# Inverse squared key norms of the RWKV-7 heads: one reciprocal per token and head, spread by TensorE, in place of one per row

## The chip, the cores and the metric

The kernel runs on one core of one Trainium2 chip. The metric is the device time of one execution in microseconds (us); the number quoted is the median of several runs.

## The reference, cut to what matters

One decoder layer: an xLSTM mLSTM group beside an RWKV-7 group, then cross-attention into a fixed memory and a SwiGLU FFN, over 2048 tokens of width 1024. The change lies in the RWKV-7 group (8 heads of 64), where the key direction is normalised per token and head:

```python
kk = hs(k * k_k)                                  # (token, head, 64)
kk = kk / jnp.maximum(jnp.sqrt(jnp.sum(kk * kk, -1, keepdims=True)), 1e-12)
a = hs(a)
k = hs(k) * (1.0 + (a - 1.0) * hp(k_a))
y = rwkv7_scan(r, hs(decay), k, v, -kk, kk * a)
```

The kernel keeps `kk` without its norm on one side of a product (`KB`) and puts the whole inverse square, 1 / max(sum, 1e-24), on the other (`RR`), so no root is taken.

## The kernel before, in words

The program runs through five stages: a pre-pass (norm, transposes, small projections, to about 118 us), the mixer (to about 1190 us), output projection, attention, and the FFN. The change touches the mixer and a constant.

`mixer` (L647) works through 16 steps: two halves of the heads (`hq`) by 8 groups of 256 tokens. For each step `prepare` (L311) runs twice, for `e` = 0 and 1, on a tile of 128 channels (two heads of 64 on the partition axis) by 256 tokens: 32 prepares in all. Beside it stand the triangular `solve` on GpSimd (L408), its `join` on TensorE (L441), the chunked `scan` (L467) and the `mlstm` group (L537), one step behind. From the second step on the big projections (`qps`, `vops` of mlstm, `kps`, `rps`, `vps` of prepare; lines 53 to 55, three fp16 passes each) are there to fill TensorE.

Channels lie on partitions, so the sum over a head's 64 channels is a matmul: `sq` (L355, ScalarE) is the squared key, and L357 multiplies it by `c.bones`, a 128x128 matrix of two 64x64 blocks of ones. That gives `sps`, in which every one of a head's 64 rows holds the same sum. VectorE then takes the maximum with 1e-24 (L359), the reciprocal (L360) and the product with `k` (L361), all on 128x256, and L364 scales the result twice into `RR`. `RR` and `KB` are the operands of `aps` (L393), whose masked copies `MX`, `RR`, `AY` (L397 to L399) feed the solve and the scan. `bps` (L379, the bonus term, `ta` from L377) and `vps` (L383, the transposed and centred `v`) share the two-buffer PSUM pool `pax` (tag `ax`) with `wps`, `sps`, `aps` and `kbps`.

A later part of each step is `tps` (L516): TensorE transposes the scan's output `y` after GpSimd has scaled it (L511, L512). `pps` (L457) is the first matmul of `join` and waits for the solve's result, fetched from DRAM as `T`.

The order of instructions on every engine is set by the scheduler of the tile framework, which simulates a timeline; each engine then runs its list in order. An edit of the source can thus move instructions well away from it.

Of the kernel before, what the change touches and what calls it, by code (L numbers as in the profile page):

```python
# [7 lines left out]
F32 = mybir.dt.float32  # L8
F16 = mybir.dt.float16
AF = mybir.ActivationFunctionType  # L10
ALU = mybir.AluOpType
# [4 lines left out]
P = 128  # L16
# [68 lines left out]
def col(c, r):  # L85
    return c.par[:, r:r + 1]
# [19 lines left out]
def rwkv_consts(c, pool, I):  # L106
    nc = c.nc
    par = c.par
    c.mu_s = pool.tile([P, 14], F32, name="mu_s")
    nc.vector.tensor_scalar(c.mu_s, par[:, R_MU:R_MU + 14], DSC, None, op0=ALU.mult)  # L110
    c.mu_c = pool.tile([P, 14], F32, name="mu_c")
    nc.vector.tensor_scalar(c.mu_c, par[:, R_MU:R_MU + 14], -DSC, DSC, op0=ALU.mult, op1=ALU.add)
    c.bones = pool.tile([P, P], F32, name="bones")
    nc.vector.memset(c.bones, 0.0)
    nc.vector.memset(c.bones[0:64, 0:64], 1.0)
    nc.vector.memset(c.bones[64:128, 64:128], 1.0)

    c.cent = pool.tile([P, P], F32, name="cent")
    nc.vector.scalar_tensor_tensor(c.cent, c.bones, -1.0 / 64, c.ident, op0=ALU.mult, op1=ALU.add)
    c.mask = pool.tile([P, P], F32, name="mask")  # L120
    nc.gpsimd.memset(c.mask, 1.0)
    for b in (0, 64):
        nc.gpsimd.affine_select(c.mask[b:b + 64, 0:64], c.mask[b:b + 64, 0:64], [[1, 64]], ALU.is_gt, 0.0,
                                base=0, channel_multiplier=-1)
        nc.gpsimd.affine_select(c.mask[b:b + 64, 64:128], c.mask[b:b + 64, 64:128], [[1, 64]], ALU.is_ge, 0.0,
                                base=0, channel_multiplier=-1)
    c.restart = pool.tile([P, 4, 64], F32, name="restart")
    nc.gpsimd.memset(c.restart, 1.0)
    nc.gpsimd.memset(c.restart[:, :, 0:1], 0.0)
    c.gmix = pool.tile([P, 8], F32, name="gmix")  # L130
    nc.vector.tensor_scalar(c.gmix, par[:, R_GMIX:R_GMIX + 8], SW, None, op0=ALU.mult)
# [115 lines left out]
def mixer_pass(c, I, hq, tp, T):  # L247

    nc, tc = c.nc, c.tc
    SGN = 256  # L250
# [35 lines left out]
    def shifted(ps, j, e, o):  # L286
        m = 4 * j + 2 * hq + e
        t = tp.t2.tile([P, SGN], F32, tag="tmu", name="tmu", bufs=2)
        nc.scalar.activation(t, ps[:, 0:SGN], AF.Copy, scale=c.mu_s[:, m:m + 1])
        nc.scalar.activation(o, ps[:, 1:SGN + 1], AF.Copy, scale=c.mu_c[:, m:m + 1])  # L290
        nc.vector.tensor_tensor(o, o, t, ALU.add)
        return o
# [18 lines left out]
    def prepare(sg, e, u, G):  # L311
# [34 lines left out]
        k = shifted(ps, 1, e, tp.t2.tile([P, SGN], F32, tag="k", name="k"))  # L346
# [6 lines left out]

        sq = tp.t1.tile([P, SGN], F32, tag="tA", name="sq")
        nc.scalar.activation(sq, k, AF.Square, scale=col(c, R_KK + ct))  # L355
        sps = tp.pax.tile([P, SGN], F32, tag="ax", name="sps")
        nc.tensor.matmul(sps, lhsT=c.bones, rhs=sq, start=True, stop=True)  # L357
        sq = tp.t1.tile([P, SGN], F32, tag="tA", name="sq")
        nc.vector.tensor_scalar(sq, sps, 1e-24, None, op0=ALU.max)  # L359
        nc.vector.reciprocal(sq, sq)  # L360
        nc.vector.tensor_tensor(sq, sq, k, ALU.mult)  # L361
        sq = sq.rearrange(v4, n=4)
        for h, b in enumerate(halves):
            nc.vector.scalar_tensor_tensor(RR[b, :, h, 0:64], sq[b], c.kk[b, 0, ct:ct + 1], E[b, :, 0:64],  # L364
                                           op0=ALU.mult, op1=ALU.mult)
# [3 lines left out]
                                       op0=ALU.mult, op1=ALU.mult)  # L369
# [257 lines left out]
    def load_u(sg):  # L627
# [13 lines left out]
    p = Ctx()  # L641
    p.weights, p.load_u, p.group, p.prepare, p.solve, p.join, p.scan, p.mlstm, p.st = \
        weights, load_u, group, prepare, solve, join, scan, mlstm, st
    return p

# [739 lines left out]
def build(tc, I, out, dbg=None):  # L1385
# [5 lines left out]
    with ExitStack() as ctx:  # L1391
# [15 lines left out]
        with ExitStack() as mix:  # L1407
            rc = mix.enter_context(tc.tile_pool(name="rc", bufs=1, side="right"))
            c.zg = rc.tile([P, 8, NC], F32, name="zg")
            rwkv_consts(c, rc, I)  # L1410
            pre_pass(c, I, T, rc)
            mlstm_gates(c, mix, I, T)
            mixer(c, I, T)
# [51 lines left out]
```

## Time and profile before

| what | us |
|---|---|
| median of 3 runs | 3042.4 (3040.26 to 3044.18) |
| the profiled execution, its own time | 3042.23 |
| its span in the profile | 3040.4 |
| TensorE busy / VectorE / ScalarE / GpSimd | 2892.4 / 2092.2 / 1251.0 / 1145.8 |

The span is what the trace covers; 1.8 us of the execution lie around it. "PE" is TensorE's matmuls, "PEld" its weight loads, DVE VectorE, ACT ScalarE, POOL GpSimd. A float32 matmul of the program shows as two records with a weight load each, so 32 `sps` matmuls are 64 records; a float32 transpose shows as one. Matmul records overlap, because the end of one is modelled with its drain; what a matmul costs TensorE is the distance from its start to the start of the next one, and not its duration.

### The profile page before, as it was taken

The page shows a single profiled execution, that of the slowest core. Times are in us where ns is not written, and L with a number is a line of the kernel's source. Part 1 is how long each engine was busy: PE and PEld are TensorE (multiplying, and loading weights), DVE is VectorE, ACT ScalarE, POOL GpSimd, SP SyncE. Part 2 cuts the span into 40 slices and gives each one's busy share as a digit, 9 for nine tenths or more (in the row PEclk, how much of TensorE's full clock was granted, in tenths as well). Part 3 has the DMA queues.
Part 4 walks back from the last instruction along what each step waited for, and adds up shares of the span by engine and source line. Part 5 has one row for each costly group of instructions (what it writes and reads, how often), then busy time and mean ns, then how long its engine had stood idle before and what let it go on. Part 6 is the DMA issues. An engine that isn't in the chain of part 4 may idle for free. (4 is left out here: it accounts for less than half of the span.)

```text
span 3040.4 us, 53763 instructions
## 1 busy us (share of the span) xinstructions
PE 2892.4 (95%) x20259; PEld 1797.2 (59%) x20259; DVE 2092.2 (69%) x3853; ACT 1251.0 (41%) x2859; POOL 1145.8 (38%) x1830
## 2 busy tenths in 40 slices
PE   7779999998999998999999998999999999899998
PEld 4568888887888887655455543444444444344443
DVE  6557777777777776564588886544545546888975
ACT  6434444555444445453466652222222223423432
POOL 3064654465555444132111153222222222644542
PEclk9889999999999999999999999999999999999999
DMA  8512222333112214554223365111111212554441
GB/s 266 141 50 62 48 50 53 83 77 88 48 46 52 50 38 129 187 177 139 87 91 132 119 245 173 56 56 56 56 59 57 61 60 70 181 180 151 156 141 72
DMA packets 328833, 307.25 MB, mean 101 GB/s; under 512 B 88846, under 2 KB 278524, under 8 KB 327676
## 3 DMA queue, kind: packets, MB, share of 16 engines
q1 hardware_dynamic: 328572, 303.81, 32.6%
q8 instruction: 160, 2.62, 0.4%
q14 instruction: 101, 0.83, 0.1%
HBM read 208.23 MB, written 95.49 MB: 100 GB/s over the span
## 5 line engine op out<-in xcount | busy, mean ns | idle before, releaser
L53 PE MATMUL pp<-u,wb 128*128 128x512 f16 x1232 | 468.2, 380 | 13.7 <-DVE e L1170 8.2
L54 PE MATMUL pp<-u,wb 128*128 128x512 f16 x1232 | 468.1, 380 | 0.0
L55 PE MATMUL pp<-u,wb 128*128 128x512 f16 x1232 | 467.9, 380 | 0.0
L1170 DVE TENSOR_TENSOR e<-pp,e 128x512 f32<-128x512 f32 x308 | 208.5, 689 | 302.3 <-PE pp L55 288.4
L432 POOL TENSOR_TENSOR tmp<-M,X 64x126 f32<-64x126 f32 (+22 forms) x496 | 193.9, 391 | 165.4 <-DMA M<-md 131.0
L55 PE MATMUL dps<-w,gS 128*128 128x512 f16 x616 | 234.1, 380 | 8.6 <-DVE gS L49 8.5
L54 PE MATMUL dps<-w,gS 128*128 128x512 f16 x616 | 234.0, 380 | 1.7 <-DVE w L49 1.7
L53 PE MATMUL dps<-w,gS 128*128 128x512 f16 x616 | 234.1, 380 | 0.0
L434 POOL TENSOR_TENSOR X<-X,tmp 64x126 f32<-64x126 f32 (+22 forms) x496 | 204.9, 413 | 35.8
L54 PEld LDWEIGHTS <-wb 128*128 128x128 f16 x1232 | 120.8, 98 | 155.3 <-issue 11.5
L53 PEld LDWEIGHTS <-wb 128*128 128x128 f16 x1232 | 120.8, 98 | 151.9 <-DMA u<-u_d 6.0
L55 PEld LDWEIGHTS <-wb 128*128 128x128 f16 x1232 | 120.8, 98 | 146.4 <-issue 1.5
L1186 POOL TENSOR_TENSOR S<-raw 128x512 f32<-128x512 f32 x22 | 33.8, 1537 | 414.2 <-DVE wb L49 414.2
L53 PE MATMUL qps<-uh,wh 128*128 128x259 f16 x512 | 141.9, 277 | 14.4 <-ACT wh L48 5.6
L54 PEld LDWEIGHTS <-wh 128*128 128x128 f16 x1280 | 128.9, 101 | 30.3 <-issue 11.6
L53 PEld LDWEIGHTS <-wh 128*128 128x128 f16 x1280 | 127.5, 100 | 25.4 <-ACT wh L48 7.0
L55 PE MATMUL qps<-uh,wl 128*128 128x259 f16 x512 | 141.1, 277 | 1.0 <-DVE wl L49 1.0
L54 PE MATMUL qps<-ul,wh 128*128 128x259 f16 x512 | 140.9, 276 | 0.0
L53 PE MATMUL vops<-wh,uh 128*128 128x256 f16 x512 | 139.7, 273 | 0.2
L55 PE MATMUL vops<-wh,ul 128*128 128x256 f16 x512 | 139.7, 273 | 0.0
L54 PE MATMUL vops<-wl,uh 128*128 128x256 f16 x512 | 139.6, 273 | 0.0
L55 PEld LDWEIGHTS <-wl 128*128 128x128 f16 x1280 | 126.4, 99 | 20.9 <-DVE wl L49 1.9
(423 smaller groups left out, 7677.2 us busy)
## 6 DMA issues: line engine op xcount, KB each, us to landing
g_d<-e SPq DMA_DIRECT2D x88, 256.0 KB
h<-h_d SPq DMA_DIRECT2D x32, 512.0 KB
acc<-h_d SPq DMA_DIRECT2D x32, 512.0 KB
u_d<-ub SPq DMA_DIRECT2D x56, 256.0 KB
wraw<-in_w_in_dram SPq DMA_DIRECT2D x48, 256.0 KB
ga<-g_d SPq DMA_DIRECT2D x32, 384.0 KB
raw<-in_ffn_w_gate_dram SPq DMA_DIRECT2D x22, 512.0 KB
raw<-in_ffn_w_up_dram SPq DMA_DIRECT2D x22, 512.0 KB
```

Source lines behind the costliest of these rows:

```text
L53: nc.tensor.matmul(out, lhsT=lhs[0], rhs=rhs[0], start=start, stop=False)
L54: nc.tensor.matmul(out, lhsT=lhs[0], rhs=rhs[1], start=False, stop=False)
L55: return nc.tensor.matmul(out, lhsT=lhs[1], rhs=rhs[0], start=False, stop=stop)
L432: nc.gpsimd.tensor_tensor(tv, M[:, s, s + 1:32].unsqueeze(2).to_broadcast(shp), X[:, s, 0:ncl].unsqueeze(1).to_broadcast(shp), ALU.mult)
L434: nc.gpsimd.tensor_tensor(X[:, s + 1:32, 0:ncl], X[:, s + 1:32, 0:ncl], tv, ALU.add)
L1170: add = lambda o, x, y: nc.vector.tensor_tensor(o, x, y, ALU.add)
L1186: nc.gpsimd.tensor_tensor(s[0], a[1][0], a[1][1], ALU.add)
```

## The change

The sums are formed the other way round: `sq` becomes the stationary operand, in two slices of 128 tokens, and a new constant `c.ind` (128x2, ones where a row belongs to the head) the moving one. `sps` is then 128 tokens by 4 (two token slices by two heads). Maximum and reciprocal run on 128x4. ScalarE repeats each value 64 times into `rcb` (128x256), and two matmuls with `rcb` as stationary operand and the identity as moving one bring it back to channels by tokens, `rb`, in PSUM. VectorE multiplies `rb` by `k`. Line numbers of the changed kernel are 4 higher from L117 on and 12 higher from L361 on.

```diff
@@ rwkv_consts
     nc.vector.memset(c.bones[64:128, 64:128], 1.0)
+    c.ind = pool.tile([P, 2], F32, name="ind")
+    nc.vector.memset(c.ind, 0.0)
+    nc.vector.memset(c.ind[0:64, 0:1], 1.0)
+    nc.vector.memset(c.ind[64:128, 1:2], 1.0)
@@ prepare
         sq = tp.t1.tile([P, SGN], F32, tag="tA", name="sq")
         nc.scalar.activation(sq, k, AF.Square, scale=col(c, R_KK + ct))
-        sps = tp.pax.tile([P, SGN], F32, tag="ax", name="sps")
-        nc.tensor.matmul(sps, lhsT=c.bones, rhs=sq, start=True, stop=True)
+        sps = tp.pax.tile([P, 4], F32, tag="ax", name="sps")
+        for m in range(2):
+            nc.tensor.matmul(sps[:, 2 * m:2 * m + 2], lhsT=sq[:, m * P:(m + 1) * P], rhs=c.ind, start=True, stop=True)
+        rc = tp.t1.tile([P, 4], F32, tag="rc", name="rc")
+        nc.vector.tensor_scalar(rc, sps, 1e-24, None, op0=ALU.max)
+        nc.vector.reciprocal(rc, rc)
+        rcb = tp.t1.tile([P, 4, 64], F32, tag="tA", name="rcb")
+        nc.scalar.copy(rcb, rc.unsqueeze(2).to_broadcast([P, 4, 64]))
+        rb = tp.pax.tile([P, SGN], F32, tag="ax", name="rb")
+        for m in range(2):
+            nc.tensor.matmul(rb[:, m * P:(m + 1) * P], lhsT=rcb[:, 2 * m:2 * m + 2].rearrange("p h d -> p (h d)"), rhs=c.ident,
+                             start=True, stop=True)
         sq = tp.t1.tile([P, SGN], F32, tag="tA", name="sq")
-        nc.vector.tensor_scalar(sq, sps, 1e-24, None, op0=ALU.max)
-        nc.vector.reciprocal(sq, sq)
-        nc.vector.tensor_tensor(sq, sq, k, ALU.mult)
+        nc.vector.tensor_tensor(sq, rb, k, ALU.mult)
```

**How the order moves, first place: TensorE and ScalarE in the second of the four prepares of steps 0 and 1.** Little is there yet to fill TensorE. `rps` and `vps` (L53 to L55) are projections of the prepare after it; `ch` belongs to the scan. TensorE before:

```order
L55 LDWEIGHTS wl
L55 MATMUL rps<-uh,wl 128x257
L473 MATMUL ch<-VS,RR_1579 64x64
L357 MATMUL sps<-sq,bones 128x256
L379 MATMUL bps<-ta,bones 128x256
L383 MATMUL vps<-cent,v 128x128 x2
L53 LDWEIGHTS wh
L53 MATMUL vps<-uh,wh 128x257
```

TensorE now:

```order
L55 MATMUL rps<-uh,wl 128x257
L485 MATMUL ch<-VS,RR_1583 64x64 x2
L362 MATMUL sps<-ind,sq 128x2 x2
L370 MATMUL rb<-ident,rcb 128x128 x2
L391 MATMUL bps<-ta,bones 128x256
L53 LDWEIGHTS wh
L53 MATMUL vps<-uh,wh 128x257
```

ScalarE now (L385 is the copy inside `KB`, L373 before):

```order
L341 ACTIVATE En<-L_1946 128x256
L345 ACTIVATE E<-L_1946 128x4x64
L359 ACTIVATE sq<-k,par 128x256
L385 COPY KB<-KB 128x4x64
L367 COPY rcb<-rc 128x256
L294 ACTIVATE r<-rps,mu_c 128x256
```

Here `rb` stands directly behind `sps` and ahead of `bps`: nothing lies between them, and `rcb` comes behind the copy inside `KB`.

**Second place: TensorE and VectorE in an `e` = 1 prepare of the second half of the heads** (the sequence repeats there from step to step). TensorE now, around `rb`; between the last `sps` and these rows stand 20 of the fp16 matmuls of `qps`, and some small ones of `join` (`xps`) and mlstm (`skp`):

```order
L55 LDWEIGHTS wl
L55 MATMUL qps<-uh,wl 128x259
L489 MATMUL ch<-R,MX_1596 128x64
L370 MATMUL rb<-ident,rcb 128x128 x2
L391 MATMUL bps<-ta,bones 128x256
L489 MATMUL ch<-R,MX_1596 128x64
L606 MATMUL ncp<-vx,Em 128x129
```

VectorE before:

```order
L587 TENSOR_TENSOR kt<-skp,tk 128x256
L372 TENSOR_TENSOR KB<-ta,En 128x4x64
L377 SCALAR_TENSOR_TENSOR ta<-r,par,ta 128x256
L359 TENSOR_SCALAR sq<-sps 128x256
L360 RECIPROCAL sq<-sq 128x256
L380 TENSOR_TENSOR bon<-bps,v 128x256
L598 SCALAR_TENSOR_TENSOR Cn<-Cn,dec,ncp 128x129
L361 TENSOR_TENSOR sq<-sq,k 128x256
L364 SCALAR_TENSOR_TENSOR RR_1582<-sq,kk,E 64x4x64 x2
```

VectorE now:

```order
L389 SCALAR_TENSOR_TENSOR ta<-r,par,ta 128x256
L625 SCALAR_TENSOR_TENSOR r<-r,ss 128x2
L364 TENSOR_SCALAR rc<-sps 128x4
L365 RECIPROCAL rc<-rc 128x4
L597 TENSOR_TENSOR Em<-Em,skp 128x256
L599 TENSOR_TENSOR kt<-skp,tk 128x256
L373 TENSOR_TENSOR sq<-rb,k 128x256
L392 TENSOR_TENSOR bon<-bps,v 128x256
L376 SCALAR_TENSOR_TENSOR RR_1586<-sq,kk,E 64x4x64 x2
```

The scheduler has put other work between `rc` and `sq` on VectorE, and between `sps` and `rb` on TensorE. From the third step on 20 to 32 fp16 matmuls stand between `sps` and `rb`, except in the two `e` = 0 prepares of steps 2 and 3, which have scan and mlstm work there. The list of DMAs (SyncE) has as many entries as before.

## Rows read from the trace of the kernel before

**Rows 1.** The page, part 1: busy time, share and records of each engine.

```profile
PE 2892.4 (95%) x20259; PEld 1797.2 (59%) x20259; DVE 2092.2 (69%) x3853; ACT 1251.0 (41%) x2859; POOL 1145.8 (38%) x1830
```

**Rows 2.** Windows: stretch, length, busy of PE, PEld, DVE, ACT, POOL; PEclk, DMA, GB/s.

```profile
120.00:200.00 80.00, 55.73 (x362) 43.89 (x361) 54.85 (x128) 32.33 (x82) 32.91 (x75) 0.83 0.32 60
245.00:575.00 330.00, 326.36 (x3535) 283.71 (x3534) 256.12 (x633) 159.72 (x469) 178.17 (x415) 1.00 0.22 52
827.00:1086.00 259.00, 245.38 (x2667) 214.04 (x2666) 191.99 (x478) 122.12 (x359) 138.16 (x319) 1.00 0.20 47
```

**Rows 3.** Waits of PE in 245 to 575 us: total us, times, longest.

```profile
PE tps L516 <- POOL y L512: 3.3, 5, 1.1
```

**Rows 4.** Waits of PE in 827 to 1110 us.

```profile
PE tps L516 <- POOL y L512: 6.2, 4, 2.0
PE qps L53 <- ACT cv L556: 4.6, 5, 1.2
PE qps L53 <- ACT r L290: 4.2, 5, 0.9
```

**Rows 5.** Waits of PE in 120 to 200 us.

```profile
PE bps L379 <- DVE ta L377: 11.3, 4, 3.3
```

**Rows 6.** Single lines, the norm: ns min/median/max of one, first and last start.

```profile
L359 DVE TENSOR_SCALAR sq<-sps x32: 393/416/425, 124.3 to 1122.5; 128x256 f32<-128x256 f32 x32
L360 DVE RECIPROCAL sq<-sq x32: 1733/1742/1753, 125.2 to 1123.0; 128x256 f32<-128x256 f32 x32
L361 DVE TENSOR_TENSOR sq<-sq,k x32: 402/420/583, 127.4 to 1125.2; 128x256 f32<-128x256 f32 x32
```

**Rows 7.** Single lines, nearest kin of the new operations.

```profile
L606 DVE RECIPROCAL r<-r x32: 144/158/167, 232.1 to 1184.8; 128x2 f32<-128x2 f32 x32
L611 DVE TENSOR_SCALAR ss<-ss x32: 157/169/279, 233.2 to 1189.8; 128x2 f32<-128x2 f32 x32
L373 ACT COPY KB<-KB x32: 404/405/425, 125.3 to 1122.1; 128x256 f32<-128x256 f32 x32
```

**Rows 8.** Timeline of PE, full mixer: start, us, engine, line, operation.

```profile
400.14 0.56 PE L477 MATMUL ch<-R,MX 128*128 128x64 f32 x4
400.54 0.28 PE L54 MATMUL qps<-ul,wh 128*128 128x259 f16 x1
400.65 0.59 PE L379 MATMUL bps<-ta,bones 128*128 128x256 f32 x2
401.08 0.61 PE L383 MATMUL vps<-cent,v 128*128 128x128 f32 x4
401.52 0.28 PE L55 MATMUL qps<-uh,wl 128*128 128x259 f16 x1
```

**Rows 9.** Timeline of PE in the pre-pass: the thinnest matmuls there.

```profile
62.42 0.17 PE L54 MATMUL gps<-wg,uh 128*128 128x8 f16 x1
62.44 0.17 PE L55 MATMUL gps<-wg,ul 128*128 128x8 f16 x1
```

**Rows 10.** Timeline of PE and DVE, second prepare, and the first join.

```profile
145.80 0.70 PE L357 MATMUL sps<-sq,bones 128*128 128x256 f32 x2 [3.17 <-ACT sq L355]
147.06 0.42 DVE L359 TENSOR_SCALAR sq<-sps 128x256 f32<-128x256 f32 x1
149.39 0.39 DVE L377 SCALAR_TENSOR_TENSOR ta<-r,par,ta 128x256 f32<-128x256 f32 x1
149.83 1.22 PE L379 MATMUL bps<-ta,bones 128*128 128x256 f32 x2 [3.33 <-DVE ta L377]
...
204.06 1.38 PE L457 MATMUL pps<-T,MX 32*32 32x32 f32 x32 [4.92 <-DMA T<-t1d]
```

**Rows 11.** Timeline of PE and DVE, a late prepare, and DVE before a late wait.

```profile
862.61 0.70 PE L357 MATMUL sps<-sq,bones 128*128 128x256 f32 x2
863.35 0.42 DVE L359 TENSOR_SCALAR sq<-sps 128x256 f32<-128x256 f32 x1
863.81 1.75 DVE L360 RECIPROCAL sq<-sq 128x256 f32<-128x256 f32 x1
869.52 1.95 PE L393 MATMUL aps<-RR,KB 128*128 128x128 f32 x16
...
908.00 0.06 DVE L340 MEMSET E<- 128x4 f32 x1 [2.47 <-POOL W L342]
```

## The prediction

> **What bounds the kernel now.** I began with the totals of the engines: TensorE is busy for 95% of the span, VectorE for 69%, ScalarE and GpSimd for about 40% [rows 1]. The change touches the mixer only, so the second view is the windows by stage. From 245 to 575 us TensorE has a matmul in flight for 326.4 of 330 us at the full granted clock of 1.00, and VectorE works for 256 us, or 78%; from 827 to 1086 us TensorE has 245.4 of 259 us and VectorE 192.0, or 74% [rows 2]. So VectorE, which the change relieves, has a fifth to a quarter of its time free in both, and TensorE, which gets more work, has almost none. In the start of the mixer, 120 to 200 us, TensorE is busy for 55.7 of 80 us at a mean clock of 0.83 [rows 2]: there chains of single operations decide.
>
> The third view says what ends TensorE's idle time. Up to 575 us it is one wait, `tps` for GpSimd's scaled `y`, 3.3 us in five steps [rows 3]. From 827 us it is 6.2 us for the same, 4.6 us for a ScalarE copy `cv` and 4.2 us for ScalarE's `r` [rows 4]. No wait for the norm, its product or `RR` is among them. The fourth view, the timeline, gives the price of a matmul as the distance between starts.
>
> **The change part by part.**
>
> VectorE. Taken away in each of 32 prepares: the maximum of 0.42 us and the reciprocal of 1.74 us [rows 6]. Added: both on 128x4, of which the nearest rows are a reciprocal on 128x2 of 0.16 us and a scalar operation on 128x2 of 0.17 us [rows 7]. The product with `k` stays at 0.42 us [rows 6], now reading `rb`. That is 2.16 - 0.33 = 1.83 us less per prepare and 59 us less in all, 3.7 us per step. I put it at nothing in the sum where TensorE is full, since VectorE has slack there [rows 2] and the waits that TensorE still has start elsewhere: before the late `r` and `tps` VectorE itself stands still, 2.47 us, for GpSimd's copy `W` [rows 11], which comes out of GpSimd's triangular solve. What it may be worth if I am wrong is a rival.
>
> ScalarE. One copy of 128x256 more, 0.41 us by its kin inside `KB` [rows 7], 13 us in all. ScalarE has half its time free [rows 2], so it costs only as part of the chain, below.
>
> TensorE. The old `sps` is one float32 matmul of 256 columns in two passes. Its twin `bps`, with the same operands' shapes, starts at 400.65 and the next matmul at 401.08: 0.43 us [rows 8]. The way back, `rb`, is two float32 matmuls of 128 columns; `vps` is the same, four passes from 401.08 to 401.52: 0.44 us [rows 8]. The new sums are four passes of 2 columns with a fresh 128x128 float32 stationary operand each. The trace has no such row, so it is bounded. The nearest is `ch` (L477), float32, the same stationary size, 64 columns: four passes from 400.14 to 400.54, 0.10 us each [rows 8]. The other end is `gps`, fp16 with 8 columns, 0.02 to 0.03 us from start to start [rows 9]. With 128 columns a pass takes 0.11 us and with 64 still 0.10 us, so a float32 pass hardly gets cheaper with fewer columns, and the load seems to set its price: I take 0.10, 0.40 us for four. At the other end it is 0.10 us for four. Hence 0.40 + 0.44 - 0.43 = +0.41 us per prepare, between +0.11 and +0.45.
>
> The Trainium skill, TensorE: Matmul & The Clock Gate, section LDWEIGHTS (loading the stationary operand), says that a load costs its number of columns over 1.2 GHz, whatever streams past it afterwards: an estimate from it of 0.107 us a pass makes +0.44 us per prepare, against the +0.11 us that `gps` would give. By that rule, the `ch` row agrees and thin matmuls are no saving here, which speaks against this change.
>
> Of the 32 prepares, 28 lie where TensorE is full, from step 2 on: 28 x 0.41 = **+11.5 us**.
>
> The chain. `rb` waits for VectorE's reciprocal and ScalarE's copy, and `bps` stands behind it in TensorE's list. In a late prepare the maximum starts 0.74 us and the reciprocal 1.20 us after `sps` [rows 11]; with the short operations `rc` is ready near 1.2 us and `rcb` 0.41 us later, say 2 us with the hand-overs. Between `sps` and `rb` the scheduler has put 20 fp16 matmuls at 0.11 us (the distance from 400.54 to 400.65 [rows 8]), 2.2 us, with small float32 ones besides. So it is covered, by one microsecond or less. And `RR`, after `rb`, has until `aps`, which came 6.9 us after `sps` before [rows 11]; I cost the chain at nothing.
>
> The start. In the four prepares of steps 0 and 1 nothing covers it. Before, `sps` starts at 145.80 and TensorE idles 3.33 us until `bps` at 149.83, because `ta` (L377) stands behind the long reciprocal on VectorE [rows 10]; the four such waits make 11.3 us [rows 5]. Now, from the maximum's start at 147.06 [rows 10]: 0.17 + one 128x256 operation of 0.42 + 0.16 on VectorE, then two copies of 0.41 on ScalarE, then `rb` with 0.44, is 149.07 without hand-overs. `bps` comes up to 0.76 us earlier, or no earlier with hand-overs and a lower clock. I take 0.5 us. Only two prepares count: behind the other two lies TensorE's wait of 4.92 us for the first solve [rows 10], which takes up what they gain. **-1.0 us**, between +2 and -2.5.
>
> What fills a wait. In steps 2 to 7 the new passes fall partly between the scan's output and `tps`, where TensorE waits for GpSimd anyway [rows 3]. At most 3.3 us come back; I take **-2.5 us**. In the second half the list between the two is no longer than before, and I take nothing of [rows 4].
>
> After the mixer no operation changes, and the four new memsets run at the start beside DMAs.
>
> The sum is +11.5 - 1.0 - 2.5 = +8.0 us on the profiled execution of 3042.2 us. That stands 0.2 us under the median of 3042.4, so 3050 us either way. A measurement here tells about 0.2% from no change, 6 us; the forecast lies just beyond it. Its own range runs from 28 x 0.11 with both gains at their fullest, 3.1 - 2.5 - 3.3 = -2.7, to 28 x 0.45 with +2 and none of the fill, +14.6: 3039 to 3057 us.
>
> **The rivals.**
>
> VectorE's relief shortens the steps: faster. If TensorE's late waits for `cv` and `r`, 8.8 us in five steps [rows 4], are owed to a late VectorE, then relief of 3.7 us per step removes them, 1.8 us in each of seven second-half steps, 12 us. With the 6.2 and 3.3 us for `tps` [rows 3, 4] that is -22 in the place of -2.5, and 11.5 - 1.0 - 22 makes about 3031 us. It decides when more than 17 us of TensorE's waits go. For it: VectorE is the second busiest engine in the mixer. Against it: before two of these waits it stood idle itself [rows 11]. Chance 0.17, at 3031 to 3036 us.
>
> TensorE has room that its busy row hides: no change. The Trainium skill, Perfetto Trace Analysis, section Identifying the Most-Contended Engine, holds matmul busy time a bad measure and the busy share of weight loads the good one. That share is 283.7 of 330 us here, 86% [rows 2]. If the added passes slip into the rest, and with the -3.5 us of the other terms, the time is about 3039; if half of them do, 3044. Against it: starts follow each other without a gap in [rows 8]. Chance 0.20, at 3038 to 3045 us.
>
> `rb` waits: slower still. Were the chain 0.5 us longer than its cover in each of 28 prepares, TensorE would stand 14 us more, with `bps` and all that follows behind it: 3064 us. It decides from a `sps` to `rcb` time of some 2.2 us on. For it: the cover is thin and VectorE runs its list in order, so one late wait ahead of `rc` is passed on. Chance 0.08.
>
> **How the numbers follow.** The forecast has 0.55. Of its range some two thirds lie more than 6 us above the time before, so slower is 0.37 + 0.08 = 0.45; same is the remaining 0.18 with the second rival's 0.20, 0.38; faster is 0.17. The range that holds 8 in 10 leaves out half of the fast rival and the upper part of the last: 3035 to 3058 us.
>
> **What would show it right or wrong.** Right: VectorE's busy time falls to about 2033 us and ScalarE's rises to 1264; four thin passes of `sps` take 0.4 us from start to start and `rb` 0.44; steps in 245 to 575 us get longer by some 0.8 us; waits of `tps` there shrink. Wrong: thin passes at 0.03 us, waits of PE for `rcb` in the full stretches, or late waits for `cv`, `r` and `tps` that are gone.

## The result, and the profile after

The changed kernel takes 3061.5 us (median of 3 runs, 3058.3 to 3062.9) where the kernel before takes 3042.4: a ratio of 1.0055, with a 95% interval of 1.0041 to 1.0068. It is slower by 19 us, above the range that was forecast. The profiled execution took 3058.3 us with a span of 3056.6, 16.2 us longer than the span before.

The page, part 1, of the changed kernel, and its windows (columns as in [rows 2]):

```profile
PE 2911.3 (95%) x20451; PEld 1822.3 (60%) x20451; DVE 2046.0 (67%) x3856; ACT 1257.4 (41%) x2891; POOL 1144.7 (37%) x1830
...
120.00:200.00 80.00, 54.14 (x368) 44.46 (x369) 46.81 (x122) 32.55 (x85) 30.95 (x71) 0.80 0.33 60
245.00:575.00 330.00, 326.07 (x3557) 286.09 (x3554) 234.76 (x629) 159.92 (x476) 172.55 (x400) 1.00 0.21 51
830.00:1090.00 260.00, 254.49 (x2723) 222.78 (x2721) 182.66 (x480) 121.96 (x368) 138.12 (x322) 1.00 0.22 53
```

VectorE is 46 us less busy, and nothing came of it; TensorE is 19 us busier and the span 16 us longer. In the full stretches TensorE has about as little idle time as before, or less. The single lines of the new operations (columns as in [rows 6]) have the durations that were taken from their kin:

```profile
L364 DVE TENSOR_SCALAR rc<-sps x32: 142/154/163, 123.6 to 1135.1; 128x4 f32<-128x4 f32 x32
L365 DVE RECIPROCAL rc<-rc x32: 161/178/178, 124.2 to 1135.3; 128x4 f32<-128x4 f32 x32
L367 ACT COPY rcb<-rc x32: 390/403/404, 124.6 to 1135.5; 128x256 f32<-128x256 f32 x32
L373 DVE TENSOR_TENSOR sq<-rb,k x32: 352/424/426, 126.3 to 1138.5; 128x256 f32<-128x256 f32 x32
```

What they cost TensorE is read from starts. Timeline of PE, a prepare in the full mixer of the changed kernel:

```profile
404.87 0.61 PE L362 MATMUL sps<-ind,sq 128*128 128x2 f32 x4
405.41 0.37 PE L475 MATMUL xps<-MX,T 32*32 32x32 f32 x10
...
409.51 0.61 PE L370 MATMUL rb<-ident,rcb 128*128 128x128 f32 x4
409.96 0.60 PE L391 MATMUL bps<-ta,bones 128*128 128x256 f32 x2
```

`sps` costs 0.54 us here (404.87 to 405.41), where the old `sps` in the same place, ahead of `xps`, cost 0.63; in the other prepares of a step it costs mostly 0.36 to 0.37 where the old one cost 0.43. `rb` costs 0.45 us here (409.51 to 409.96), and 0.45 to 0.69 in the 28 prepares, by what follows it. Added up from start to start over these 28, `sps` and `rb` take 26.3 us where the old `sps` took 15.1: 11.2 us more, 0.40 per prepare. The forecast said 11.5 and 0.41.

The waits of PE in the changed kernel, in 120 to 200 us, in 245 to 575 us and in 830 to 1110 us (total us, times, longest):

```profile
PE sps L362 <- ACT sq L359: 13.7, 4, 4.6
PE rb L370 <- ACT rcb L367: 6.8, 4, 1.9
PE aps L405 <- ACT VS L398: 3.2, 1, 3.2
...
PE rb L370 <- ACT rcb L367: 1.5, 4, 0.6
PE tps L528 <- POOL y L524: 1.5, 1, 1.5
PE aps L405 <- ACT VS L398: 0.9, 3, 0.4
...
PE tps L528 <- POOL y L524: 2.7, 4, 0.8
PE aps L405 <- DVE AY L411: 1.3, 3, 0.6
PE ch L485 <- DVE VS L502: 0.9, 2, 0.5
```

In the kernel before, `sps` waited in 120 to 200 us like this:

```profile
PE sps L357 <- ACT sq L355: 10.8, 4, 3.2
```

In the start, the four waits of `bps` [rows 5] are gone, 11.3 us, but `rb` waits for 6.8, `sps` for 13.7 where it waited for 10.8 before, and one `aps` for 3.2. From 245 us `tps` gave up 1.8 of its 3.3 us [rows 3], and `rb` and `aps` took 2.4. In the second half the 15 us of `tps`, `cv` and `r` [rows 4] have shrunk to about 5.

The `aps` row of the start leads to ScalarE. Its timeline there, in the kernel before:

```profile
129.60 1.09 ACT L386 COPY VS<-vps 64x128 f32<-64x128 f32 x4 [0.59 <-PE vps L383]
131.85 0.69 ACT L583 ACTIVATE Em<-mb,tk 128x128 f32<-128x128 f32 x2 [1.17 <-DMA mb<-m_d]
```

and in the changed kernel, with TensorE's rows that follow:

```profile
136.18 0.69 ACT L595 ACTIVATE Em<-mb,tk 128x128 f32<-128x128 f32 x2 [8.91 <-DMA mb<-m_d]
136.90 1.08 ACT L398 COPY VS<-vps 64x128 f32<-64x128 f32 x4
...
138.04 1.16 PE L405 MATMUL aps<-RR,KB 128*128 128x128 f32 x8 [3.23 <-ACT VS L398]
...
149.15 1.01 PE L362 MATMUL sps<-ind,sq 128*128 128x2 f32 x4 [4.60 <-ACT sq L359]
151.75 1.23 PE L370 MATMUL rb<-ident,rcb 128*128 128x128 f32 x4 [1.59 <-ACT rcb L367]
152.77 1.06 PE L391 MATMUL bps<-ta,bones 128*128 128x256 f32 x2
```

`VS` and `Em` have changed places in ScalarE's list. `Em`, a piece of mlstm that the change does not touch, waits 8.91 us for a DMA, and the copies `VS` stand behind it, some 4 us after they could have run (e2, below, has them at 132.83 us); so `aps` is late, and the second prepare's `sps` comes at 149.15 us and not at 145.80 [rows 10]. Within a prepare the change does what was forecast: `sps` to `bps` is 3.62 us, 0.4 less than before.

Over the mixer the changed kernel falls behind like this (start of the last `vops` matmul of a step): 3.4 us at 218, 5.0 at 276, 10.5 at 545, 10.7 at 734, 15.2 at 1171. The start can be told from the rest by marks inside one execution. From the first `sps` to the first `sps` of step 2 it is 122.2 us in the kernel before and 128.0 in the changed one, 5.8 us more; from the last `vops` at 276 us to the one at 1119 us it is 843.3 and 852.4 us, 9.1 more.

### The profile page after: what moved, and what is told of

Its sections match the earlier page's. It is cut to its first block, busy times and chain, and to the rows that moved or that the text cites. A ratio compares the mean times of both kernels' runs of the same rounds, so it can differ in the third digit from the quotient of the medians.

```text
span 3056.6 us, 54229 instructions
## 1 busy us (share of the span) xinstructions
PE 2911.3 (95%) x20451; PEld 1822.3 (60%) x20451; DVE 2046.0 (67%) x3856; ACT 1257.4 (41%) x2891; POOL 1144.7 (37%) x1830
## 5 line engine op out<-in xcount | busy, mean ns | idle before, releaser
L53 PE MATMUL pp<-u,wb 128*128 128x512 f16 x1232 | 467.5, 379 | 12.8 <-DVE e L1182 9.1
L55 PE MATMUL pp<-u,wb 128*128 128x512 f16 x1232 | 467.4, 380 | 0.0
L55 PE MATMUL dps<-w,gS 128*128 128x512 f16 x616 | 233.4, 379 | 9.4 <-DVE gS L49 9.4
L53 PE MATMUL dps<-w,gS 128*128 128x512 f16 x616 | 233.5, 379 | 0.0
L53 PEld LDWEIGHTS <-wb 128*128 128x128 f16 x1232 | 120.7, 98 | 149.8 <-DMA u<-u_d 4.2
L55 PEld LDWEIGHTS <-wb 128*128 128x128 f16 x1232 | 120.6, 98 | 146.0 <-issue 0.7
L1198 POOL TENSOR_TENSOR S<-raw 128x512 f32<-128x512 f32 x22 | 33.8, 1537 | 408.7 <-DVE wb L49 408.7
L53 PE MATMUL qps<-uh,wh 128*128 128x259 f16 x512 | 142.9, 279 | 4.5 <-ACT r L294 2.2
L54 PEld LDWEIGHTS <-wh 128*128 128x128 f16 x1280 | 128.9, 101 | 23.5 <-issue 6.0
L55 PE MATMUL qps<-uh,wl 128*128 128x259 f16 x512 | 141.7, 278 | 1.2 <-DVE wl L49 1.2
L53 PEld LDWEIGHTS <-wh 128*128 128x128 f16 x1280 | 129.1, 101 | 20.3 <-ACT wh L48 1.2
L53 PE MATMUL vops<-wh,uh 128*128 128x256 f16 x512 | 139.7, 273 | 0.5 <-ACT cv L568 0.5
L55 PEld LDWEIGHTS <-wl 128*128 128x128 f16 x1280 | 127.3, 100 | 21.2 <-DVE wl L49 1.8
L55 PE MATMUL vops<-wh,ul 128*128 128x256 f16 x512 | 139.7, 273 | 0.0
```

What stands on the lines that cost most here:

```text
L53: nc.tensor.matmul(out, lhsT=lhs[0], rhs=rhs[0], start=start, stop=False)
L54: nc.tensor.matmul(out, lhsT=lhs[0], rhs=rhs[1], start=False, stop=False)
L55: return nc.tensor.matmul(out, lhsT=lhs[1], rhs=rhs[0], start=False, stop=stop)
L1198: nc.gpsimd.tensor_tensor(s[0], a[1][0], a[1][1], ALU.add)
```

## The experiments

Each run stands beside runs of the kernel before on the same chip. The last column is the ratio less one, times 3044 us, the middle of the medians of before.

| run | ratio (95%) | us against before |
|---|---|---|
| e1 changed kernel again | 1.0056 (1.0044 to 1.0068) | +17.0 |
| e2 `Em` held | 1.0046 (1.0034 to 1.0058) | +14.0 |
| e3 four more passes, free order | 1.0102 (1.0089 to 1.0115) | +31.0 |
| e4 no reciprocal, free order | 1.0017 (1.0008 to 1.0025) | +5.2 |
| e5 old work, new order | 1.0087 (1.0073 to 1.0100) | +26.5 |
| e6 new work, old order | 1.0111 (1.0095 to 1.0126) | +33.8 |
| e7 four more passes, old order | 1.0011 (1.0002 to 1.0020) | +3.3 |
| e8 no reciprocal, old order | 0.9994 (0.9985 to 1.0003) | -1.8 |
| e9 new order, no wait for `rb` | 1.0072 (1.0058 to 1.0086) | +21.9 |
| e10 e9 without `rb` | 1.0032 (1.0019 to 1.0044) | +9.7 |
| e11 new work, old order, `rb` by hand | 1.0026 (1.0015 to 1.0037) | +7.9 |
| e12 lines moved in the source | 1.0029 (1.0017 to 1.0040) | +8.8 |
| e13 as e11, buffers too | 1.0031 (1.0020 to 1.0043) | +9.4 |
| e14 four more passes, new order | 1.0089 (1.0075 to 1.0103) | +27.1 |
| e15 eight more passes, old order | 1.0043 (1.0031 to 1.0056) | +13.1 |
| e16 e12 with `Em` held | 1.0018 (1.0009 to 1.0027) | +5.5 |

**First group: one part at a time.** The changed kernel again, and with `Em` of step 0 tied behind the first copies `VS`:

> The changed kernel once more, as the base for the others of this group. Theory M: the loss of 19 us is 3.4 us in the start, where ScalarE's Em now stands ahead of the copies VS, about 12 us of added TensorE passes paid in full, and a small rest; 3058 to 3063 us, +16 to +21 us over the kernel before. The same is expected by every rival; a figure under +14 us would mean that the first comparison was a stray one.

> The changed kernel, with the first Em of the mixer put back behind the first prepare's copies VS in ScalarE's order; nothing else moves on TensorE or VectorE. Theory M: the second prepare's sps starts at 145.8 us again instead of 149.2, and 3.4 us of it last to the end: 3.4 us under the changed kernel, between 2.5 and 4. Rival A (the delay would have been absorbed by the wait for the first solve, which was 4.92 us long before): no difference, within 1 us. Rival B (reordering of ScalarE is most of the loss, TensorE's passes little): more than 8 us come back.

```diff
-nc.scalar.copy(VS[halves[1 - h], o::2, h], vps[halves[o], :, 64 * h:64 * h + 64])
+g.vs = nc.scalar.copy(VS[halves[1 - h], o::2, h], vps[halves[o], :, 64 * h:64 * h + 64])
...
+with tc.issue_after(st.hold.ins) if sg == 0 and hq == 0 and e == 0 else nullcontext():
```

Then TensorE's added time alone, and VectorE's relief, each put into the kernel before. The second of them, e4, also holds `Em` behind `VS`, with the lines of e2 above, so it is not the relief alone:

> The kernel before, with two more float32 matmuls of 128 columns in each prepare (into sps, whose old product then overwrites them; the result is the reference's). TensorE gets four passes of 0.11 us more per prepare, 0.44 us, VectorE and ScalarE nothing, and no chain gets longer. Theory M (added TensorE time is paid in full where TensorE is full): 28 prepares x 0.44 = +12.3 us, between +10 and +14. Rival C (TensorE has room that its busy row hides): 0 to +5 us. Rival D (added passes fall partly into waits): +8 to +10 us.

```diff
+for m in range(2):
+    nc.tensor.matmul(sps[:, m * P:(m + 1) * P], lhsT=c.ident, rhs=sq[:, m * P:(m + 1) * P], start=True, stop=True)
 nc.tensor.matmul(sps, lhsT=c.bones, rhs=sq, start=True, stop=True)
```

> The kernel before with the reciprocal left out: the maximum also multiplies by a constant, so the keys are scaled by a wrong factor, and the output is not the reference's. VectorE has 1.74 us less in each of 32 prepares, 56 us in all; TensorE and ScalarE keep their work. Theory M (VectorE's relief is worth little in the full stretches): the start gets 1 to 3 us shorter, the rest 0 to 3 us; -1 to -5 us in all. Rival E (VectorE's relief shortens the steps): -8 us or more, up to -22. Rival F (VectorE's relief is worth nothing or delays other work): 0 to +3 us.

```diff
-nc.vector.tensor_scalar(sq, sps, 1e-24, None, op0=ALU.max)
-nc.vector.reciprocal(sq, sq)
+nc.vector.tensor_scalar(sq, sps, 1e-24, 1e-12, op0=ALU.max, op1=ALU.mult)
```

The loss repeats. With `Em` held the median is 3.3 us lower, as theory M had it, though the intervals overlap; the trace (timelines of ScalarE and TensorE) shows the mechanism, and that it is not all of the start:

```profile
132.83 1.09 ACT L398 COPY VS<-vps 64x128 f32<-64x128 f32 x4 [4.19 <-PE vps L395]
...
148.02 1.01 PE L362 MATMUL sps<-ind,sq 128*128 128x2 f32 x4 [4.60 <-ACT sq L359]
```

From the first `sps` to the second it is 22.7 us in the kernel before, 26.8 in the changed one, 24.0 here; what is left is the longer wait for `sq` (4.60 where it was 3.17). To the first `sps` of step 2 it is 122.2, 128.0 (128.9 in e1) and 124.0 us.

The other two broke theory M and its rivals alike. Fourteen us of added TensorE time cost 31, and 56 us less of VectorE cost 5: neither price can be that of the work. In both the scheduler had put the mixer into another order. In e3 the trace shows what that order costs: the waits of PE from 276 to 1150 us, first in the kernel before and then in e3.

```profile
PE tps L516 <- POOL y L512: 11.7, 11, 2.0
...
PE qps L53 <- ACT cv L558: 22.4, 12, 5.6
PE tps L518 <- POOL y L514: 15.7, 10, 2.4
PE qps L53 <- ACT r L290: 11.4, 12, 1.2
```

`cv` and `r` took 4.6 and 4.2 us before [rows 4], so these three waits grew by 29 us. That became **theory N**: an edit of some tenths of a us reorders the mixer, and the order alone is worth several us.

**Second group: order held.** The kernels of this group build two programs. The first gives the order of every engine; in the second each instruction that both have is tied behind its neighbour of that order, with edges that set the issue order and bring no wait of their own:

```python
for row in order.values():
    row = [at[k] for k in row if k in at]
    for a, b in zip(row, row[1:]):
        tc.add_manual_dep(b, a.name, dep, reason="order")
```

Instructions that only one of them has are placed by the scheduler. The computation is edited as above. In the traces of e5 to e8 the shared instructions of TensorE, ScalarE and GpSimd stand in exactly the sequence that was asked for, and those of VectorE but for one small `MEMSET`.

> The computation of the kernel before, with every instruction that both kernels have held in the order in which it stands in the changed kernel, on every engine. What differs from the kernel before is the order alone. Theory N (formed after the first four runs: an edit that gives VectorE less or TensorE more also makes the scheduler reorder the mixer, and the order alone costs or gains several us): +4 to +10 us over the kernel before, 3.4 us of it in the start. Theory M (the loss is TensorE's passes and the start): +3 to +4 us. Rival G (the new order is made for short VectorE operations and the long reciprocal now blocks it): over +12 us. Rival H (order is worth nothing): 0.

> The changed computation, with every instruction that both kernels have held in the order of the kernel before; the added ones (second sps, the copy rcb, rb) are placed by the scheduler. Theory M: 28 x 0.42 = +11.8 us over the kernel before, between +9 and +14, since TensorE's passes are paid in full and the start keeps its order. Theory N: the same. Rival G': in the old order the product with k stands close behind the reciprocal, so VectorE waits for rb there, and TensorE for what VectorE holds back: over +18 us.

> The kernel before with two more float32 matmuls of 128 columns per prepare, as in the run with the same edit before, and now with everything else held in the order of the kernel before. TensorE gets four passes of 0.11 us more per prepare, 0.44 us. Theories M and N: 28 to 32 x 0.44 = +12 to +14 us; the other 17 to 19 us of the earlier +31 came from the reordering. Rival I (TensorE's time costs more than itself, because every wait behind it gets longer): +25 us or more again. Rival C (TensorE has hidden room): under +6 us.

> The kernel before with the reciprocal left out (the keys are scaled by a wrong factor), as in the earlier run, and now with everything else held in the order of the kernel before. VectorE has 1.74 us less per prepare, 56 us in all. Theory N: -3 us in the start and 0 to -6 us after it, -3 to -9 us in all; the +5 us of the earlier run came from the reordering. Theory M: -1 to -5. Rival E (VectorE's relief is worth 12 us or more): -12 or below. Rival F (no gain from it): 0 to +3.

With the order held, the passes that had cost 31 us cost 3.3, and the missing reciprocal that had cost 5.2 gains 1.8, with an interval that holds zero. So 28 and 7 us of the first group were order. For e7 theories M and N had both said 12 to 14 us; the figure is that of rival C, room on TensorE. The passes were there. Timeline of PE, four more passes in the old order:

```profile
371.12 0.61 PE L420 MATMUL sps<-sq,ident 128*128 128x128 f32 x4
371.56 0.60 PE L421 MATMUL sps<-sq,bones 128*128 128x256 f32 x2
372.00 0.27 PE L94 MATMUL kps<-uh,wh 128*128 128x257 f16 x1
```

The slot is 0.88 us where it was 0.43 to 0.44, so 0.44 us were added, 14 us in 32 prepares. The waits of PE from 245 to 575 us show where part of them went:

```profile
PE tps L583 <- POOL y L579: 1.4, 4, 0.7
```

`tps` waited for 3.3 us there before [rows 3]; 1.9 us of the 4.8 that 11 prepares added there fell into it. More than that is not seen in this execution, which took 3050.9 us, 2.8 over the median of its eleven: from 276 to 1119 us it is 9.8 us longer than the profile of before, and the listed waits of PE there fell from 36.9 to 34.6 us. That the passes cost 3.3 rests on the medians.

The crossed runs both fared worse than either kernel. The old work in the new order (+26.5, rival G) has its 1.74 us reciprocal in a VectorE list made without one. The new work in the old order (+33.8, rival G') has `rb` where the scheduler placed it, and TensorE stands for it. Its waits of PE from 245 to 575 us, from 830 to 1110 us, and in all from 276 to 1150 us:

```profile
PE rb L413 <- ACT rcb L410: 4.5, 5, 1.4
...
PE rb L413 <- ACT rcb L410: 9.6, 8, 2.1
...
PE rb L413 <- ACT rcb L410: 22.6, 17, 2.8
```

Each order is worse with the other's work than with its own, so e5 and e6 can't be added up to the result.

**Third group: the place of `rb`, the chain, the passes in the new order.**

> The changed kernel in its own order, with one thing left out: the product with k reads k and a constant in place of rb, so that VectorE and RR no longer wait for sps, rc, rcb and rb (the norm is left out of the keys; all its operations still run). Theory N1 (the detour over rcb and rb makes RR and aps later, by 1.0 to 1.4 us per prepare, and the mixer pays for it): 5 us or more come back, +14 or less over the kernel before. Theory N2 (the order itself costs, wherever rb comes): within 3 us of the changed kernel, +14 to +20 us.

```diff
-nc.vector.tensor_tensor(sq, rb, k, ALU.mult)
+nc.vector.scalar_tensor_tensor(sq, k, 1e-12, k, op0=ALU.mult, op1=ALU.mult)
```

> As the run that leaves the norm out of the product, and without the two rb matmuls: TensorE has 0.44 us less in each of 32 prepares, in the order of the changed kernel. Against the run that keeps rb: theory N (in a fixed order waits take up most of a few more passes, as the run with more passes in the old order showed): 2 to 6 us less. Theory M (passes are paid in full): 12 to 14 us less. With N2 the time stays 10 us or more over the kernel before; with N1 it comes within 8 us of it.

```diff
-for m in range(2):
-    nc.tensor.matmul(rb[:, m * P:(m + 1) * P], lhsT=rcb[:, 2 * m:2 * m + 2].rearrange("p h d -> p (h d)"), rhs=c.ident,
-                     start=True, stop=True)
```

> The changed computation once more in the order of the kernel before, now with rb placed by hand on TensorE, where rcb is ready by the trace of the kernel before (rec + 0.95 us after sps, some 17 to 29 matmuls behind sps), and vps of the same prepare 12 matmuls behind it; in the source rb's PSUM buffer is asked for behind bps, so that bps may stay early. All else is as before. Theory N (what costs is a place where TensorE waits for rcb, or where rb comes too late; the passes themselves cost little): +3 to +10 us over the kernel before, in the place of +32. Rival (the detour costs whatever its place, because VectorE's list stands still behind the product): over +20 us.

```diff
+RB_AT = [4, 2, 2, 2, 43, 57, 16, 37, 27, 36, 24, 38, 27, 36, 26, 41, 17, 37, 78, 36, 25, 27, 20, 17, 20, 17, 22, 17, 20, 17, 22, 17]
...
+j = row.index(("sps0", n + 1)) + RB_AT[n]
+row[j:j] = [("rb0", n + 1), ("rb1", n + 1)]
```

> The changed kernel with the lines from rcb to RR moved down in the source, behind the bonus product and ahead of vps; the work is the same, the scheduler orders it freely, and rb's PSUM buffer is asked for behind that of bps. Theory N (the same work in another order is worth several us either way): it differs from the changed kernel by more than 4 us, on either side. Theory M (the time follows from the work): within 3 us of the changed kernel, +14 to +20 us over the kernel before.

```diff
-        rcb = tp.t1.tile([P, 4, 64], F32, tag="tA", name="rcb")
...
         nc.vector.tensor_tensor(G.bon[:, e], bps, v, ALU.mult)
+        rcb = tp.t1.tile([P, 4, 64], F32, tag="tA", name="rcb")
...
         vps = tp.pax.tile([P, 2, P], F32, tag="ax", name="vps")
```

That VectorE waits for `rb` is not what costs: without this wait the time is no shorter. The median of e9 is 5 us over the changed kernel, which none of the theories had, but the two intervals overlap. TensorE's own wait for `rcb` is still there in e9 (6.9 us in the start, 1.6 from 245 to 575 us); e10 takes it away together with the passes. There 12 us go against e9 and 7 against e1, for 14 us of passes: theory M's figure against e9, and not the 2 to 6 of theory N. So in the new order half of a pass or more is paid.

e11 is the changed computation in the old order, with `rb` where the trace says it fits, and costs +7.9 us and not +33.8. e12 is the same computation as the changed kernel, again ordered freely, and differs from it in the place of twelve lines of source: +8.8 us and not +17. Both are theory N's outcome, and neither interval reaches that of e1. Since e12 is ordered freely, its gain is that of all that moved, and is not pinned to one instruction.

**Fourth group: closing it.**

> As the run with rb placed by hand in the order of the kernel before, with one repair. There the lag grew by 4.4 us (from 1.9 to 6.3) between the steps at 545 and 591 us, where rb came 8.6 us after sps, held behind bps by the order in which the two ask for a PSUM buffer. Now rb asks ahead of bps in the 10 prepares in which it is to come first. Theory O (order and work are apart: the work of the change costs 3 to 4 us, as four more passes do in the old order, and the rest of the loss is the order): +2 to +6 us over the kernel before. Rival P (the new work costs about +8 us in any order): +7 to +10 us.

```diff
+late = not EARLY[NOW["n"]]
+if not late:
+    back(sq, rc)
...
 nc.vector.tensor_tensor(G.bon[:, e], bps, v, ALU.mult)
-back(sq, rc)
+if late:
+    back(sq, rc)
```

Here `back` stands for the lines from `rcb` to `RR`.

> The changed kernel in its own order, with two more float32 matmuls of 128 columns per prepare (the identity with itself, into rb's buffer, which rb then overwrites), 0.44 us each time, 14 us in all. Theory Q (in the new order no wait takes passes up, as the run without rb showed with 12 us for 0.44 us per prepare): +10 to +15 us over the changed kernel, +27 to +32 over the kernel before. Rival R (a pass costs about a quarter in either order, and the 12 us were a shift of the waits): +2 to +6 us over the changed kernel.

```diff
+for m in range(2):
+    nc.tensor.matmul(rb[:, m * P:(m + 1) * P], lhsT=c.ident, rhs=c.ident, start=True, stop=True)
```

> The kernel before in its own order with four more float32 matmuls of 128 columns per prepare, 0.88 us each time, 28 us in all, where the run with two more (14 us) cost 3.5 us. Theory S (the waits of TensorE take up some 10 us in all, and are used up): +14 to +20 us. Rival R (a pass costs about a quarter): +6 to +9 us.

```diff
-for m in range(2):
+for m in range(4):
```

> The changed kernel with the lines from rcb to RR moved down behind the bonus product, freely ordered, and the first Em held behind the first copies VS, as in the second run: the best of the changed computation without an order written by hand. If the two effects add, 8.8 - 3.3 = +5 to +6 us over the kernel before; if the hold is worth nothing here, +8 to +10 us.

Its edit is that of e12 and that of e2 together.

e13 misses: in its trace the jump is smaller (5.2 to 7.1 us), but its time is not shorter, and rival P has it. The repair also moved `rb` to another place in eleven prepares. With the old order and `rb` placed by hand, e11 and e13 agree on +8 to +9 us.

e14 and e15 bear out that the price of a pass hangs on the order. In the new order 14 us more cost 10, with 4 to 16 left by the intervals of e1 and e14; the added passes stand up to 5 us ahead of `rb` there, and so also hold its buffer from then on. In the old order the first 14 us cost 3.3 and the next 14 cost 9.8, in all just under theory S's range and over rival R's. That they fill TensorE's waits is seen in part: from 276 to 1119 us the listed waits of PE are 36.9 us before, 34.6 in e7 and 31.3 in e15, and `tps` from 245 to 575 us is down from 3.3 us [rows 3] over 1.4 to this, in e15:

```profile
PE tps L583 <- POOL y L579: 0.9, 1, 0.9
```

e16 adds the two cures, and they add as expected: +5.5 us, the best of the changed computation. Its start (timelines of ScalarE and TensorE) has `VS` ahead of `Em` and the second `sps` in time:

```profile
130.90 1.08 ACT L398 COPY VS<-vps 64x128 f32<-64x128 f32 x4 [3.71 <-PE vps L395]
135.52 0.69 ACT L596 ACTIVATE Em<-mb,tk 128x128 f32<-128x128 f32 x2 [3.53 <-DMA mb<-m_d]
...
145.70 0.92 PE L362 MATMUL sps<-ind,sq 128*128 128x2 f32 x4 [4.60 <-ACT sq L359]
```

From the first `sps` to the first of step 2 it takes 122.1 us, as much as the kernel before (122.2), where e12 takes 126.5. But for `Em` and the mask behind it, the two run their instructions in one sequence.

No version was faster than the kernel before; e8 says that, in the old order, there was next to nothing to win on VectorE. Its waits of PE from 830 to 1110 us still have those for `cv` and `r` [rows 4], no shorter:

```profile
PE qps L94 <- ACT cv L623: 6.0, 5, 2.0
PE qps L94 <- ACT r L336: 4.5, 5, 1.0
```

## Why the prediction was wrong, step by step

It had the right sign and the right cause for part of the loss, and a sum of +8.0 us where +16.2 (the profiled pair) to +19.1 (the medians) came.

- **VectorE at nothing: right.** e8 takes 56 us off VectorE with the order held and gains 1.8 us, between 4.6 gained and 0.9 lost. The rival of 3031 us falls. One sign that was to show the forecast wrong did come: in the changed kernel the late waits for `cv` and `r` are gone from 830 to 1110 us. But they stayed in e8, which has the relief and the old order, and in e11 (3.7 and 3.5 us); they went with the order.
- **TensorE, +11.5 us: right in size.** Four thin passes cost 0.36 to 0.37 us mostly (0.40 was taken), `rb` 0.45 to 0.69 (0.44 was taken), and the whole comes to 11.2 us in 28 prepares. That they are paid in full held only nearly, and only in the order that came: 7 to 12 of 14 us there (e10), 10 of 14 in e14; in the old order it was 3.3 of 14 (e7).
- **The chain at nothing: right.** `rb` waits for 1.5 us from 245 to 575 us and does not appear from 830 us on; the rival of 3064 us, near in its number, fails by its mechanism.
- **The start, -1.0 us: the step that failed, and the largest miss.** Its inner part was right (`bps` came 0.4 us earlier behind `sps`), but the step looked at TensorE and VectorE alone, and took the order of ScalarE's list as it was. There `Em` had moved ahead of `VS`. From the first `sps` to the first of step 2 the changed kernel takes 5.8 us more than the kernel before, and 6.7 in e1, in the place of 1.0 less; with `Em` held 1.8 are left (e2). Holding `Em` brings back 3.0 us (e1 to e2) and 3.3 (e12 to e16) by the ratios, and 4.0 to 4.9 in the start by the traces of these pairs.
- **The fill, -2.5 us: failed.** `tps` gave up 1.8 us from 245 to 575 us, but new waits of `rb` and `aps` took 2.4. In the old order passes cost less than themselves, by more than forecast (e7: 14 us of passes for 3.3).
- **What no step had: the order itself.** From 276 to 1119 us the changed kernel takes 9.1 us more than the kernel before, and 11.7 in e1, close to the 9.0 that the passes and the fill were to make. That is luck in part. The listed waits of PE there fell by 8 to 10 us (36.9 to 27.0, and 29.1 in e1) and not by 2.5, and about as much went into longer distances between starts, too short to be listed as waits, which are not traced to a cause. That much of the loss is order and not work is shown by e11, e12, e13 and e16: the same computation in other orders costs 5.5 to 9.4 us. Which of the moved instructions hold it, beyond `Em`, stays open.
- **The rival that TensorE has room** (0.20) was half right: by the medians the kernel before has 10 to 15 us of room in its own order (14 - 3.3 in e7, 28 - 13.1 in e15), and the new order has less of it (14 - 10.1 in e14).

So the forecast of +8 priced the work, which costs 5.5 to 9.4 us in the better orders; it took the order around it for fixed.

## What to carry to other kernels

Where a scheduler sets the order, price an edit twice: the work with the order held, by tying every old instruction to its old neighbour, and then what the scheduler made of it; here the second was about as large as the first. Look through the lists of all engines for an instruction that waits for a DMA and has moved ahead of ready work, and for the order in which tiles ask for a shared PSUM buffer: holding `Em` behind `VS`, and moving `rb`'s lines so that it asks for its buffer behind `bps`, gave back 11 of 17 us (e16), though what else moved with the lines has its part in that. And time added to the busiest engine can be cheap at first and dear next: 3.3 us for the first 14 in the old order, 9.8 for the next.

## What was not expected of the hardware

Two executions of the same program do not place their time alike. At the end of the mixer the changed kernel was 15.2 us behind the profile of before in one execution and 20.6 in the other (e1), with 2 us between their total times. A single pair of profiles can't place a loss of a few us; the medians of many runs, and a mechanism that repeats in several traces such as `Em` ahead of `VS`, can.

Busy time falls by less than the operations that go: taking away 32 reciprocals of 1.74 us, 56 us, lowered VectorE's busy row by 41 us in e4 (2092.2 to 2051.1) and by 46 in e8 (2045.9), and ScalarE's rose by 6.4 us for 32 copies of 0.40 us in the changed kernel. Why is not shown here.
